# Two decoder layers on one core: slots by age, later low parts of the value weights, fp32r transposes of gathered rows

## The chip, the core and the metric

The kernel runs on one core of one Trainium2 chip. The core has a matmul engine (TensorE, PE in the profile, with its weight loads as PEld), a vector engine (VectorE, DVE), an activation engine (ScalarE, ACT), GpSimd (POOL) and a queue engine (SyncE, SP) that only issues DMAs here. The metric is the device time of one execution in microseconds. Three executions of the kernel before took 1535.93, 1536.97 and 1539.32 us; their median, 1536.97 us, is the time before.

## What is computed

Two layers over 512 tokens of width 1024. Each layer mixes tokens by two attentions that run on the same projection, and then sends each token through 2 of 16 experts:

```python
for l in range(DEPTH):
    mix = token_mixer(x, w_in[l], ...)      # selected sparse attention + stick-breaking attention
    x = layer_norm(DN_ALPHA * x + mix, ln1_g[l], ln1_b[l])
    ffn = grouped_moe(x, w_router, router_bias, exp_w_gate[l], exp_w_up[l], exp_w_down[l])
    x = layer_norm(DN_ALPHA * x + ffn, ln2_g[l], ln2_b[l])
...
def grouped_moe(...):
    scores = sigmoid(xf @ w_router)          # choose one group of 4 experts, then 2 of them
    for e in range(N_EXPERTS):
        h = silu(xf @ exp_w_gate[e]) * (xf @ exp_w_up[e])
        y = y + combine[:, e:e + 1] * (h @ exp_w_down[e])
```

All arithmetic is float32.

## The kernel before

**Products in three terms.** TensorE multiplies in the format fp32r, which holds fewer bits than float32. Each operand is therefore split in two (`Chip.split`): ScalarE copies it to an fp32r tile (the high part, line 484), and VectorE subtracts that from the original into a second fp32r tile (the low part, line 495). A product is three matmuls (`mm3`): low x high, high x low, high x high. So each weight tile of 128 x 1024 (two blocks of 512 columns, 512 KB) costs one DMA on SP, one ScalarE cast, one VectorE subtraction and its matmuls. The helpers record every operation, so in the profile nearly all VectorE work has line 495, all ScalarE casts line 484, all matmuls line 447 and all transposes line 445; tile names and times tell them apart. `s` are tiles in SBUF, `m` small ones (a few bytes per partition), `p` and `a` PSUM banks.

**The planner sets the order.** The program is first recorded as a list of operations with their dependencies (`Recorder.add`), each with an assumed duration and a priority, which is its place in the list, moved forward by `R.bump` for loads and splits of weights. `Recorder.plan` then simulates the five engines: at each step the engine that is free first takes the ready operation of the lowest priority number. The result is one order per engine, and the operations are emitted in it. A dependency that is added by hand (`o.deps.add`) acts in this simulation and so on the order; the emitted program waits only for what data and buffers need.

**Slots.** All working tiles share fixed slots: 48 in SBUF for kind `s`, 56 for `m`, 4 PSUM banks each for `p` and `a`. When an operation writes a new tile, `take` (in `plan`) picks a slot that is free at that time of the simulation. Before the change it is the one that came free last: `s` is sorted by the time of release, and the index is the largest one whose time has passed. In the emitted program the first writer of the new tile waits for the last users of the old tile in that slot, whenever they end on the chip. Groups have quotas: 46 slots for loads of expert weights (`x`), 24 for their split parts (`ew`), 2 for gathered rows (`xg`), 6 for their transposed parts (`xh`). The DMA queue SP works in order, so a load that waits for its slot holds back the loads behind it.

**A layer.** First come projections and the two attentions, then the output projection with the first normalisation and the router (`out_proj`, `route_tile`). The normalised rows go to DRAM (`x1d`), and a copy to `zd`, into which the experts add. Per expert (`moe`): GpSimd gathers the expert's rows from `x1d` (`gather`, line 1179) into a tile `xg`; TensorE transposes it in 8 blocks of 128 x 128 (`transpose_tile`, by an identity matrix `ident`); the 8 blocks are split; gate and up take 24 matmuls of 512 columns each (8 blocks in three terms), the two halves of down 12 each, 72 in all; GpSimd adds the scaled result to `zd` by an indirect DMA (`add_rows`, line 1184). Expert 0 has its rows from matmuls instead of a gather. Before the last expert stands a branch for overfull experts (`overflow`), not taken here, that reserves a number of tiles.

**Between the layers.** `ln2` reads `zd`, adds the last expert by matmuls, normalises the four tiles of 128 tokens, and transposes and splits each for the next layer (`x2t`). The first tile (t = 0) has its statistics from VectorE (`bn_stats`), the others from ScalarE. Meanwhile the next layer's first weights are loaded and split: those of the indexer (`indexer`) and the value weights of the second attention (`vb_by_tile`, four splits k2 = 0..3). In layer 1 the indexer and the value projection run tile by tile behind `ln2`.

Of the kernel before, what the change touches and what calls it, by code (L numbers as in the profile page):

```python
# [11 lines left out]
F = mybir.dt.float32  # L12
FR = mybir.dt.float32r
# [4 lines left out]
OP = mybir.AluOpType  # L18
# [4 lines left out]
P = 128  # L23
S = 512
D = 1024
# [28 lines left out]
class View:  # L54
# [19 lines left out]
    def real(self):  # L74
        x = self.buf.tile
        for f, a, k in self.chain:
            x = getattr(x, f)(*a, **k)
        return x
# [13 lines left out]
class Recorder:  # L92
# [82 lines left out]
    def plan(self):  # L175
# [93 lines left out]
        def take(o, t):  # L269
            for b in o.allocs:  # L270
                s = slots[b.kind]
                s.sort()
                i = max((j for j in range(len(s)) if s[j][0] <= t + 1e-9), default=0)
                b.slot = s.pop(i)[1]
                g = b.group
                if g is not None:
                    if live[g] >= self.QUOTA[g]:
                        heapq.heappop(glive[g])
                        live[g] -= 1
                    live[g] += 1  # L280
                    turn[g].pop()
# [3 lines left out]
        while done < len(self.ops):  # L285
            best = None
            for e in engs:
# [3 lines left out]
                t = free[e] if ready[e] else (pend[e][0][0] if pend[e] else None)  # L291
                if t is not None and (best is None or t < best[0]):
                    best = (t, e)
            if barrier and not any(p.prio < barrier[0].prio for e in engs for p in [x[3] for x in pend[e]] + [x[2] for x in ready[e]] if p.prio < barrier[0].prio):
                o = barrier.pop()
                t = max([o.ready] + [free[x] for x in engs if x != "SP"])
# [3 lines left out]
                t = w  # L300
                e = "ALL"
# [118 lines left out]
class Chip:  # L420
# [13 lines left out]
    def mm(self, out, terms, start, stop, transpose=None, also=()):  # L434
        dt = {F: 4, FR: 1, BF: 1}
        n = self.n(out)
        if transpose is not None:
            dur = 0.11
        else:
            dur = sum(max(dt[x.dtype if not isinstance(x, View) else x.ap.dtype] * n, 256) / 2400 + 0.004 for _, x in terms)  # L440

        def fn():
            o = real(out)
            if transpose is not None:
                self.nc.tensor.transpose(o, real(transpose[0]), transpose[1])  # L445
            for i, (w, x) in enumerate(terms):
                self.nc.tensor.matmul(o, real(w), real(x), start=start and i == 0, stop=stop and i == len(terms) - 1)  # L447
        reads = [x for t in terms for x in t] + ([transpose[0]] if transpose else [])
        o = self.r.add("PE", dur, fn, [out], reads, allocs=also)
        o.cols = sum(n * w.shape[0] / P for w, _ in terms) + n * (transpose is not None)  # L450
        o.cnt = sum(2 if (x.ap.dtype if isinstance(x, View) else x.dtype) == F else 1 for _, x in terms) + (transpose is not None)
        return o
# [91 lines left out]
def build(tc, x0, xT0, w_idx, w_main, w_br, w_out, w_exp, bgate, idxg, idxb,  # L544
          ln1g, ln1b, ln2g, ln2b, wrt, rbias, ln1c, hconst, tab0, out):
    nc = tc.nc
    with ExitStack() as ctx:
# [17 lines left out]
        C = Chip(R)  # L565


        ident = const.tile([P, P], F, name="ident")
        make_identity(nc, ident)
        identb = const.tile([P, P], BF, name="identb")  # L570
        nc.vector.tensor_copy(identb, ident)
        jp = const.tile([P, P], I32, name="jp")
# [28 lines left out]
        def s4(shape, dtype=F, group=None, reserve=0):  # L601
            return R.buf("s", shape, dtype, group, reserve)
# [10 lines left out]
        wr = const.tile([P, KD, NE], F, name="wr")  # L613
        rb = const.tile([P, NE], F, name="rb")
        lnc = const.tile([P, DEPTH, 2, KD], F, name="lnc")
        onesf = const.tile([P, P], F, name="onesf")
        nc.vector.memset(onesf, 1.0)
        loaded = []
        bias_t = const.tile([P, 256 + 384 + 512], BF, name="bias")
# [19 lines left out]
        def load_w(src, k0, n=512, group="raw", reserve=0, load="w", fine=False):  # L639
            t = s4([P, 2, n], F, group, reserve)  # L640
            if fine:
                for k in range(2):
                    C.dma(t[:, k, :], src[:, (k0 + k) * n:(k0 + k + 1) * n], P * 4 * n, load=load)
                return t
            C.dma(t, src[:, k0 * n:(k0 + 2) * n].rearrange("p (k n) -> p k n", k=2), P * 8 * n, load=load)
            return t

        def split_w(raw, n=512, group="w", after=None, fine=False):
            h = s4([P, 2, n], FR, group)
            w = s4([P, 2, n], FR, group)  # L650
            if fine:
                for k in range(2):
                    C.split(h[:, k, :], w[:, k, :], raw[:, k, :])
                return [(h[:, i, :], w[:, i, :]) for i in range(2)]
            o = C.split(h, w, raw)
            if after is not None:
                o.deps.add(after)
            return [(h[:, i, :], w[:, i, :]) for i in range(2)]
# [17 lines left out]
            for n in range(2):  # L676
                C.stt(dst[:, half(n)], dst[:, half(n)], rstd, b[:, half(n)], OP.mult, OP.add)

        def transpose_tile(src, dst_of):
            for hb in range(2):  # L680
                ps = bank("a")
                for k in range(4):
                    c = (hb * 4 + k) * P
                    C.tr(ps[:, k * P:(k + 1) * P], src[:, c:c + P], ident)
                dst_of(hb, ps)

        def proj_tok(l, xT, c, done, before=None):
# [255 lines left out]
        def vb_by_tile(l, xT, vt):  # L943
            R.bump += BUMP
            w = []
            for k2 in range(4):
                w += split_w(load_w(w_main[l, M_VB, k2 // 2], 2 * (k2 % 2)), group="wo")
            R.bump -= BUMP

            def tile_of(t):  # L950
                ts = slice(t * P, (t + 1) * P)
                ps = bank("p")
                for k in range(KD):
                    C.mm3(ps, xT[k][0][:, ts], xT[k][1][:, ts], *w[k], k == 0, k == KD - 1)
                evac_v([ps], vt)
            return tile_of
# [220 lines left out]
        def gather(dst, idx, also, skip):  # L1177
            kw = dict(bounds_check=S - 1, oob_is_err=False) if skip else {}
            R.add("POOL", 1.04, lambda: nc.gpsimd.indirect_dma_start(  # L1179
                out=real(dst), out_offset=None, in_=x1d, in_offset=IOA(ap=real(idx), axis=0), **kw),  # L1180
                [dst], [idx], rtok=[f"x1{t}" for t in range(NT)], nbytes=P * (2048 if skip else 4096), allocs=also)
# [58 lines left out]
        def moe(l, tb, gl, mci, loads, xacc, until, routed):  # L1240
            def prep(e):
                xh, xl = s4([P, KD, P], FR, "xh"), s4([P, KD, P], FR, "xh")

                def dst(hb, ps):
                    ks = slice(hb * 4, hb * 4 + 4)
                    C.split(xh[:, ks, :], xl[:, ks, :], ps.rearrange("p (k t) -> p k t", k=4))
                if e == 0:
                    xg = s4([P, D], group="xg")
                    C.copy(xg[:, half(0)], xacc[0])
                    C.v("tensor_copy", xg[:, half(1)], xacc[1])  # L1250
                    transpose_tile(xg, dst)
                    return xh, xl
                xg = s4([P, D], group="xg")
                last = e == NE - 1
                gather(xg, gl[:, 0:1] if last else tb[:, e, 0:1], [xh, xl], not last)
                transpose_tile(xg, dst)
                return xh, xl

            def weights(e, i):
# [131 lines left out]
        def ln2(l, x2t, tail):  # L1391
            acc, oh, yo = tail
            R.bump += LNB
            lg, lb = load_ln(ln2g[l], ln2b[l])
            R.bump -= LNB
            for t in range(NT):
                ts = slice(t * P, (t + 1) * P)
                r = acc[t]
                ps = [bank("a" if x2t is None and t > 1 else "p") for _ in range(2)]
                for n in range(2):  # L1400
                    C.mm(ps[n], [(ident, r[:, half(n)])], True, False)
                for n in range(2):
                    C.mm(ps[n], [(oh[:, t, :], y[:, half(n)]) for y in yo], False, True)
                if t:
                    mean, rstd = stats_by_act(r, ps)
                else:
                    bs, mv = sm([P, 2, 6]), sm([P, 2])
                    for n in range(2):
                        C.v("bn_stats", bs[:, n, :], ps[n], n=512)
                    rstd, mean = norm_of(mv, bs, LN_EPS / ALPHA ** 2), mv[:, 0:1]  # L1410
                for n in range(2):
                    C.stt(r[:, half(n)], ps[n], mean, lg[:, half(n)], OP.subtract, OP.mult)
                for c in (half(0), half(1)) if t == 0 else (slice(0, D),):
                    C.stt(r[:, c], r[:, c], rstd, lb[:, c], OP.mult, OP.add)
                C.dma((out if l == DEPTH - 1 else x2d)[ts, :], r, P * 4096, wtok=[f"x2{t}"])
                if x2t is not None:
                    def dst(hb, ps):
                        for k in range(2):
                            h, w = x2t[hb * 2 + k]
                            C.split(h[:, :, ts], w[:, :, ts], ps[:, k * 256:k * 256 + 256].rearrange("p (k t) -> p k t", k=2))  # L1420
                    transpose_tile(r, dst)

        def x_tiles():
            x2 = [(s4([P, 2, S], FR), s4([P, 2, S], FR)) for _ in range(KD // 2)]
# [165 lines left out]
```

## Time and profile before

| | |
|---|---|
| median of three executions | 1536.97 us |
| the profiled execution | 1539.54 us |
| its span, first to last instruction | 1537.7 us |
| mean granted TensorE clock | 0.983 |
| read from HBM, written | 293.80 MB, 28.46 MB |
| loads of expert weights | 384 of 512 KB |
| gathers, scatter-adds | 30, 30 |

How it is read: a row of a timeline has the start in us from the span's start, its length in us, engine, line, operation, output <- inputs, shape and count, and in brackets the idle time of the engine before it and what ended that. A row of groups has count, busy us and mean ns of one, then the idle time before. A row of waits reads "engine, output, line <- what it waited for: us in total, times, longest". A row of stretches has busy us and number of instructions for PE, PEld, DVE, ACT and POOL, then the granted clock, the DMA share and GB/s. Neighbouring instructions of one kind are merged in a timeline, so that a row can hold several with their count.

The layers lie in the span as follows: attention of layer 0 to about 360 us, projection and routing to 470, experts to 745; layer 1 attention to about 1120, projection and routing to 1225, experts to 1510; the last normalisation to the end.

### The profile page before, as it was taken

Reading aid. Unit: us, or ns where it says so; the run is one execution under the profiler, and the core shown is the slowest. Engines: PE = TensorE matmul, PEld = TensorE weight load, DVE = VectorE, ACT = ScalarE, POOL = GpSimd, SP = SyncE. Lnnn points to the kernel's source line nnn. Section 1 sums busy time; section 2 is a strip of 40 time slices with the busy share of each in tenths; the row PEclk is TensorE's granted clock in tenths of the full one; section 3 lists DMA queues with packets and bytes.
Section 4 is the critical chain, followed back from the end, with each engine's and each line's share of the span. In section 5 each row is a group of like instructions: output and inputs, shape, how many; then the busy total and the mean of one; then the engine's idle time right before and its main releaser. Section 6 shows DMA issues by size and latency. Waiting matters only on the chain. (4 is left out here: it accounts for less than half of the span.)

```text
span 1537.7 us, 21018 instructions
## 1 busy us (share of the span) xinstructions
PE 1475.2 (96%) x7188; PEld 1178.9 (77%) x7188; DVE 1249.5 (81%) x2301; ACT 896.6 (58%) x1459; POOL 142.4 (9%) x127
## 2 busy tenths in 40 slices
PE   8999999999989999999799999999999899999985
PEld 7877777777867878888588777777778578888874
DVE  5699996777587989999765999867766789999975
ACT  4335543675146878888623455446831478888873
POOL 0000000000031131210010000000001212112110
PEclk9999999999999999999999999999999899999998
DMA  6221112117888989999712221221287889999962
GB/s 217 71 91 57 68 56 89 63 42 288 302 280 297 337 309 348 341 334 333 237 61 69 83 61 50 82 83 55 70 306 279 302 307 351 341 352 339 351 216 108
DMA packets 91265, 308.52 MB, mean 201 GB/s; under 512 B 15439, under 2 KB 15567, under 8 KB 91152
## 3 DMA queue, kind: packets, MB, share of 16 engines
q1 hardware_dynamic: 82000, 290.69, 53.5%
q0 software_dynamic: 9152, 16.43, 4.5%
q8 instruction: 58, 0.95, 0.2%
q14 instruction: 55, 0.45, 0.1%
HBM read 293.80 MB, written 28.46 MB: 210 GB/s over the span
## 5 line engine op out<-in xcount | busy, mean ns | idle before, releaser
L447 PE MATMUL p<-s,s 128*128 128x512 f32 (+1 forms) x5192 | 1268.1, 398 | 28.1 <-DVE s L495 25.7
L447 PEld LDWEIGHTS p<-s,s 128*128 128x128 f32 x5192 | 952.9, 191 | 234.9 <-DVE s L495 25.5
L495 DVE TENSOR_TENSOR s<-s,s 128x1024 fp32r<-128x1024 f32 (+2 forms) x526 | 612.1, 1195 | 152.4 <-ACT s L484 112.3
L484 ACT CAST s<-s 128x1024 fp32r<-128x1024 f32 (+2 forms) x526 | 518.2, 1029 | 226.6 <-PE p L447 141.6
L495 DVE TENSOR_TENSOR s<-a,s 128x256 fp32r<-128x256 f32 (+3 forms) x386 | 169.5, 479 | 36.5 <-ACT s L484 32.7
L484 ACT CAST s<-a 128x256 fp32r<-128x256 f32 (+2 forms) x354 | 127.1, 414 | 109.8 <-PE a L445 103.7
L445 PE MATMUL a<-ident,s 128*128 128x128 f32 x888 | 134.0, 277 | 13.5 <-DMA s<-x1d,m 6.4
L445 PEld LDWEIGHTS a<-ident,s 128*128 128x128 f32 x888 | 106.7, 142 | 44.9 <-issue 11.5
L523 POOL TENSOR_TENSOR m<-m,nhalf 128x1 f32<-128x1 f32 x24 | 17.8, 741 | 891.0 <-DVE m L495 881.6
L480 ACT ACTIVATE s<-a 128x512 f32<-128x512 f32 (+3 forms) x156 | 61.9, 450 | 46.0 <-PE a L447 27.5
L484 ACT COPY s<-a 64x512 f32<-64x512 f32 (+1 forms) x48 | 27.8, 583 | 96.7 <-PE a L445 45.3
L1184 POOL DMA_INDIRECT zd<-s,m x30 | 61.1, 2035 | 199.8 <-ACT s L487 167.4
L487 ACT ACTIVATE s<-p,m 128x512 f32<-128x512 f32 (+1 forms) x64 | 44.1, 689 | 53.5 <-PE p L447 50.6
L1179 POOL DMA_INDIRECT s<-x1d,m x30 | 43.6, 1452 | 267.9 <-PE p L447 220.2
L464 PE MATMUL a<-s,s 64*128 64x384 f32 (+3 forms) x456 | 67.4, 351 | 0.0
L447 PEld LDWEIGHTS a<-s,s 128*128 128x128 f32 x360 | 57.0, 188 | 9.2 <-issue 2.2
L447 PE MATMUL a<-s,s 128*128 128x324 f32 (+4 forms) x360 | 62.2, 321 | 1.5 <-DVE s L495 1.3
L464 PEld LDWEIGHTS a<-s,s 64*128 64x128 f32 x456 | 41.3, 185 | 27.6 <-issue 20.4
L495 DVE MAX8 m<-s 128x8 f32<-128x256 f32 (+2 forms) x96 | 53.4, 556 | 1.8
L495 DVE MATCH_REPLACE8 s<-m,s 128x256 f32<-128x256 f32 (+2 forms) x96 | 52.0, 542 | 0.0
L495 DVE TENSOR_TENSOR_SCAN s<-s 128x128 f32<-128x128 f32 (+3 forms) x64 | 51.0, 812 | 0.1
L484 ACT CAST s<-p 128x512 fp32r<-128x512 f32 x48 | 27.9, 588 | 38.5 <-DVE p L495 22.7
(107 smaller groups left out, 632.4 us busy)
## 6 DMA issues: line engine op xcount, KB each, us to landing
s<-in_w_exp SPq DMA_DIRECT2D x384, 512.0 KB
s<-in_w_main SPq DMA_DIRECT2D x79, 512.0 KB
s<-in_w_br SPq DMA_DIRECT2D x16, 512.0 KB
s<-in_w_out SPq DMA_DIRECT2D x16, 512.0 KB
x1d<-s SPq DMA_DIRECT2D x8, 512.0 KB
zd<-s SPq DMA_DIRECT2D x8, 512.0 KB
s<-zd SPq DMA_DIRECT2D x8, 512.0 KB
s<-in_w_idx SPq DMA_DIRECT2D x8, 324.0 KB
```

The costliest lines, as they stand in the source:

```text
L445: self.nc.tensor.transpose(o, real(transpose[0]), transpose[1])
L447: self.nc.tensor.matmul(o, real(w), real(x), start=start and i == 0, stop=stop and i == len(terms) - 1)
L464: self.nc.tensor.matmul(real(o), real(t[i][0]), real(t[i][1]), start=i == 0, stop=stop and i == len(t) - 1)
L480: self.nc.scalar.activation(real(out), real(src), func, bias=real(bias), scale=real(scale), **kw)
L484: return self.r.add("ACT", 0.1 + self.psum(out, src) + self.n(out) * 0.833e-3, lambda: self.nc.scalar.copy(real(out), real(src)), [out], [ ...
L487: return self.r.add("ACT", 0.2 + self.n(out) * 0.833e-3, lambda: self.nc.scalar.mul(real(out), real(src), real(c)), [out], [src, c])
L495: getattr(self.nc.vector, method)(real(out), *[real(a) for a in args], **{k: real(x) for k, x in kw.items()}, **({} if accum is None else ...
L523: return self.r.add("POOL", 0.47, lambda: self.nc.gpsimd.tensor_tensor(real(out), real(a), e, OP.pow), [out], [a])
L1179: R.add("POOL", 1.04, lambda: nc.gpsimd.indirect_dma_start(out=real(dst), out_offset=None, in_=x1d, in_offset=IOA(ap=real(idx), axis=0), * ...
L1184: rows = R.add("POOL", 1.04, lambda: nc.gpsimd.indirect_dma_start(out=zd, out_offset=IOA(ap=real(idx), axis=0), in_=real(src), in_offset=None,
```

## The change

Three edits, and a constant that goes with the third:

- `take` uses the slot that has been free longest (index 0 of the sorted list) for every kind but `m`.
- In `vb_by_tile` the low parts of the value weights k2 = 1, 2, 3 depend on the last operation of the first tile's normalisation in `ln2`, kept in the list `first_tile`.
- The gathered rows are written to an fp32r tile (as raw float32 bytes), and their transposes use an fp32r identity; the PSUM output is viewed in the same type. All other transposes use the same bytes viewed as float32.
- The identity is made in the buffer `onesf`, copied by VectorE to the fp32r tile, and `onesf` is set to ones afterwards.

```diff
@@ take
-                i = max((j for j in range(len(s)) if s[j][0] <= t + 1e-9), default=0)
+                i = max((j for j in range(len(s)) if s[j][0] <= t + 1e-9), default=0) if b.kind == "m" else 0
@@ mm
-                self.nc.tensor.transpose(o, real(transpose[0]), transpose[1])
+                self.nc.tensor.transpose(o.bitcast(transpose[1].dtype), real(transpose[0]), transpose[1])
@@ constants
-        ident = const.tile([P, P], F, name="ident")
-        make_identity(nc, ident)
+        onesf = const.tile([P, P], F, name="onesf")
+        make_identity(nc, onesf)
+        identr = const.tile([P, P], FR, name="identr")
+        nc.vector.tensor_copy(identr, onesf)
+        ident = identr.bitcast(F)
...
-        onesf = const.tile([P, P], F, name="onesf")
         nc.vector.memset(onesf, 1.0)
@@ transpose_tile
-        def transpose_tile(src, dst_of):
+        def transpose_tile(src, dst_of, by=ident):
...
-                    C.tr(ps[:, k * P:(k + 1) * P], src[:, c:c + P], ident)
+                    C.tr(ps[:, k * P:(k + 1) * P], src[:, c:c + P], by)
@@ vb_by_tile
                 w += split_w(load_w(w_main[l, M_VB, k2 // 2], 2 * (k2 % 2)), group="wo")
+                if k2:
+                    R.ops[-1].deps.add(first_tile[-1])
@@ moe, prep
-                xg = s4([P, D], group="xg")
+                xg = s4([P, D], FR, group="xg")
                 last = e == NE - 1
-                gather(xg, gl[:, 0:1] if last else tb[:, e, 0:1], [xh, xl], not last)
-                transpose_tile(xg, dst)
+                gather(xg.bitcast(F), gl[:, 0:1] if last else tb[:, e, 0:1], [xh, xl], not last)
+                transpose_tile(xg, dst, identr)
@@ ln2
                 for c in (half(0), half(1)) if t == 0 else (slice(0, D),):
-                    C.stt(r[:, c], r[:, c], rstd, lb[:, c], OP.mult, OP.add)
+                    o = C.stt(r[:, c], r[:, c], rstd, lb[:, c], OP.mult, OP.add)
+                if t == 0:
+                    first_tile.append(o)
...
+        first_tile = []
```

## The prediction, made before the change was run

> **What bounds the kernel now.** I read the page first, then busy times by stretches, then the waits, then the timeline around each long wait.
>
> ```profile
> PE 1475.2 (96%) x7188; PEld 1178.9 (77%) x7188; DVE 1249.5 (81%) x2301; ACT 896.6 (58%) x1459; POOL 142.4 (9%) x127
> ```
>
> TensorE (PE) is busy for 96% of the 1537.7 us span, so time is won in two ways only: work taken off PE, or PE stalls taken away. A stretch inside the experts of layer 0 shows how closely the others follow (busy us of PE, PEld, DVE, ACT, POOL; then granted clock, DMA share, GB/s):
>
> ```profile
> 560.00:580.00 20.00, 20.00 (x86) 16.39 (x85) 17.60 (x18) 16.03 (x20) 3.57 (x2) 0.88 0.88 292
> ...
> 600.00:620.00 20.00, 20.00 (x96) 16.70 (x95) 18.75 (x19) 17.32 (x21) 4.56 (x3) 1.00 0.98 347
> ```
>
> In the steady state PE has no idle time, DVE 1.25 us in 20, and the DMA engines are full as well. The first row is the same work with the clock at 0.88. Three stretches show where that comes from:
>
> ```profile
> 557.90:564.80 6.90, 6.24 (x15) 4.88 (x16) 6.39 (x6) 6.80 (x9) 2.05 (x1) 0.51 0.63 218
> 742.30:745.70 3.40, 2.94 (x16) 2.54 (x14) 3.22 (x4) 1.68 (x3) 0.00 (x0) 0.50 0.77 278
> 1496.60:1503.40 6.80, 3.49 (x15) 3.19 (x15) 4.19 (x5) 2.94 (x3) 0.00 (x0) 0.50 0.22 77
> ```
>
> After a stall PE runs at half clock for 3.4 or 6.8 us, so a stall costs more than its gap. What the stalls wait for:
>
> ```profile
> ACT s L484 <- DMA zd<-s,m: 17.0, 10, 6.6
> ```
> ```profile
> SPq L526 <- DVE s L495: 816.8, 213, 34.8
> ```
>
> The first row (us in total, times, longest): ScalarE, about to write the high part of a weight, waits for a scatter-add into zd. No weight depends on zd; what can tie the two is the SBUF slot: the planner gives out the slot that came free last, and that slot's last user is still being read by the scatter, or is tied to it. The second row is the DMA queue's own: nearly every load is held by a slot that VectorE has only just let go.
>
> **The change, part by part.** *Slots by age.* No instruction is added or moved by this; each new tile takes the slot that has been free longest in the plan, so its wait is for older work. Three stalls carry the gain. The first:
>
> ```profile
> 556.21 2.94 ACT L484 CAST s<-s 128x1024 fp32r<-128x1024 f32 x3 [6.64 <-DMA zd<-s,m]
> ...
> 557.30 0.50 PE L447 MATMUL p<-s,s 128*128 128x512 f32 x1 [1.81 <-ACT s L484]
> ```
>
> ScalarE stands 6.64 us and PE loses 1.81. The half clock behind it lets 6.24 us of busy time do 0.51 of its work: 6.24 x 0.49 = 3.06. Together 4.9. The second and the third:
>
> ```profile
> 739.72 1.23 DVE L495 TENSOR_TENSOR s<-s,s 128x1024 fp32r<-128x1024 f32 x1 [3.15 <-DMA zd<-s,m]
> ...
> 741.33 3.48 PE L447 MATMUL p<-s,s 128*128 128x256 f32 x18 [3.87 <-DVE s L495]
> ```
> ```profile
> 1498.12 3.68 DVE L495 TENSOR_TENSOR s<-s,s 128x1024 fp32r<-128x1024 f32 x3 [6.45 <-DMA zd<-s,m]
> ...
> 1499.40 3.36 PE L447 MATMUL p<-s,s 128*128 128x256 f32 x14 [5.12 <-DVE s L495]
> ```
>
> At 741 the low part could start once its high part is cast; I give PE 2.6 of the 3.87 us, and of the half clock 2.94 x 0.5 = 1.5: 4.1. At 1499 VectorE was free 6.45 us earlier, more than PE's gap, so all 5.12 go, and 3.49 x 0.5 = 1.75 of clock: 6.9. Sum 15.9. Ends: 0 if the wait is a dependency and not the slot, 17.1 with the whole 3.87. I take nearly the upper end, since a weight's split has no data from zd. What is late next is the split itself, then the load. The loads cost PE nothing directly: they may only be issued earlier. Tiles of kind m keep the old rule.
>
> The Trainium skill (TensorE: Matmul & The Clock Gate, "What's actually happening") gives the half clock to an idle 3413 ns window; the three rows agree in length and depth. By its rule the clock terms (6.3 of the 15.9) return only where no such window stays idle; without them the sum is 6.3 smaller.
>
> *fp32r transposes.* 30 gathers (15 experts, 2 layers) give 8 transposes each, 240 of the 888. Their pace now, in a group of 12 (4 of another kind and these 8), against single durations:
>
> ```profile
> 585.89 1.47 PE L445 MATMUL a<-ident,s 128*128 128x128 f32 x12
> 603.57 1.47 PE L445 MATMUL a<-ident,s 128*128 128x128 f32 x12
> ```
> ```profile
> L445 PE MATMUL a<-ident,s 128*128 128x128 f32 x888 | 134.0, 277 | 13.5 <-DMA s<-x1d,m 6.4 <-DVE s L495 4.8 <-DVE m L495 0.9
> L445 PEld LDWEIGHTS a<-ident,s 128*128 128x128 f32 x888 | 106.7, 142 | 44.9 <-issue 11.5 <-DVE s L495 9.6 <-DMA s<-x1d,m 3.4
> ...
> L447 PE MATMUL a<-s,s 128*128 128x384 f32 x64 | 16.4, 337 | 0.0
> ...
> L447 PE MATMUL a<-s,s 128*128 128x256 f32 x64 | 12.8, 282 | 0.0
> ```
> ```profile
> 407.91 0.96 PE L447 MATMUL a<-k,s 128*128 128x16 f32 x8
> ```
>
> Pace: (1470 - 277) / 11 = 108 ns. A transpose of 128 columns lasts 277 ns, as long as an fp32r matmul of 256 columns (282): fp32 streams its identity twice. One pass of 128 columns is 337 - 282 = 55 ns. The other limit is the weight load. The router's 16-column matmuls, which stream next to nothing, still come about 0.1 us apart, so an ordinary four-byte load takes that long; the transposes' loads are shorter (142 ns). Lower end: one pass, about 58 ns. Upper end: the fp32r transpose's load is an ordinary one, and the pace stays 108 (or 112, a loss of 1 us in all). I take 58, because the transpose's load is already of the short kind. In each 8 the last is followed by an ordinary load that binds anyway, so 7 count: 30 x 7 x 50 ns = 10.5 us, all on PE, which has no idle time there.
>
> The same page ("Terms") calls transpose mode four times faster for FP32. The trace does not show that at 108 ns, twice one pass of 55; if the fp32r identity brings it out, the term would be 30 x 7 x 53 ns = 11.1.
>
> *Low parts after the first tile.* Three VectorE subtractions of the next value weights move behind the first tile's last step; no DMA goes with them, and the dependency is in the plan alone, so nothing waits on a new semaphore.
>
> ```profile
> 755.68 1.21 DVE L495 TENSOR_TENSOR s<-s,s 128x1024 fp32r<-128x1024 f32 x1
> ...
> 758.65 1.17 DVE L495 TENSOR_TENSOR s<-s,s 128x1024 fp32r<-128x1024 f32 x1
> ...
> 759.81 1.40 DVE L495 SCALAR_TENSOR_TENSOR s<-p,m,s 128x512 f32<-128x512 f32 x2
> ...
> 765.71 2.48 PE L447 MATMUL a<-s,s 128*128 128x324 f32 x15 [1.33 <-DVE s L495]
> ...
> 772.89 4.92 PE L447 MATMUL p<-s,s 128*128 128x512 f32 x21
> ```
>
> The first and the last of the three are shown, 1.2 us each. They stand between the first tile's statistics and its normalisation (759.81): 3.6 us. Between 0 (latencies fill the room) and 3.6 comes back at the index matmul of 765.71; below nothing, one of them in front of the transposed tile's split costs 1.2. I take 2.0. Their own reader is the matmul at 772.89, 7 us after that one: this hides them. If that cover were gone, 1.2 us each would be paid.
>
> The extra identity copy at the start is one small VectorE operation while it waits for the first loads: nothing, or at most itself.
>
> *Sum.* 15.9 + 10.5 + 2.0 = 28.4, less 1.0 that the loads may take back (second rival): 27.4. The profiled execution took 1539.54 (span 1537.7 and 1.8 around it), 2.57 above the median of 1536.97. 1539.54 - 27.4 = 1512.1; on the median's footing 1509.5.
>
> **The rivals.** *No faster transpose:* the load binds at 108 ns. For it stand the router's matmuls, against it the 142 ns. 1509.5 + 10.5 = 1520.
>
> *The loads become the bound:*
>
> ```profile
> q1 hardware_dynamic: 1763, 6.41, 87.9%
> ```
>
> This row is of 600 to 620: 6.41 MB in 20 us at a DMA share of 0.98. An expert needs 12 x 512 KB = 6.29 MB, so 19.6 us, while PE takes 17.7 (603.57 - 585.89). PE already eats into a lead. If that lead is nearly gone, what is saved among the experts (10.5 + 4.9) is waited for again, and 741, 1499 and the boundary stay: 4.1 + 6.9 + 2.0 = 13.0, so 1524. Against it: no PE wait on an expert load stands among the waits, and 560 to 580 (DMA at 0.88 behind the stall) fills up again. The Trainium skill (DMA: Bandwidth & Descriptors, "Where 436 GB/s comes from") puts a core's HBM limit at about 358 GB/s; the 347 above agree, and no earlier issue would lift them.
>
> *Slower: the gathers come late.* Free slots let the queue run ahead, more loads are in flight, and each gather shares the engines with them.
>
> ```profile
> 593.12 1.04 POOL L1179 DMA_INDIRECT s<-x1d,m  x1 [9.73 <-PE p L447]
> ```
> ```profile
> DMA to landing us min/median/max: 5.7/6.8/7.8
> ```
>
> A gather is issued 603.57 - 593.12 = 10.4 us before its transposes and lands after 6.8. From 10.4 on, each microsecond costs 30; from about 11.3 the gain is used up. At 12 us: 30 x 1.6 = 48 more, 1557. Against it: the engines are full now as well, and the gathers, held 9.73 us by a slot, start earlier too.
>
> *It does not do what it says:* zd is waited for in earnest and the transposes keep their pace: 2 us of gain less 1, 1536.
>
> **How the numbers follow.** Forecast 0.55 (1500 to 1517 by its terms' ends), no faster transpose 0.22, loads 0.11, no change 0.05, slower 0.07. A measurement of this kernel can tell about 0.2%, 3 us, from no change. The range 1500 to 1527 takes in the first three. Faster 0.88, same 0.05, slower 0.07.
>
> **What would show it.** Right: no wait on zd left in ScalarE's and VectorE's rows; the clock at 1.00 in the experts; group of 12 in about 1.1 us; the index matmul of the second layer without its 1.33 us; most loads no longer held by VectorE. Wrong: the group still 1.47; PE waiting for loads of expert weights or for gathers; a stall of 5 us before the last expert's last matmuls; the low parts in front of the transposed tile's split.

## The result, and the profile after

Four executions of the changed kernel took 1510.46 to 1514.59 us, median 1514.01, beside 1538.14 for four of the kernel before: a ratio of 0.9836 (95% interval 0.981 to 0.9862). The forecast was 1509.5, its range 1500 to 1527. The profiled execution took 1514.59 (span 1512.9), 24.95 us less than the 1539.54 of before; the sum of the forecast was 27.4.

The busy times on the page of the changed kernel, then three stretches from its view by windows:

```profile
PE 1464.2 (97%) x7188; PEld 1172.2 (77%) x7188; DVE 1242.4 (82%) x2302; ACT 890.9 (59%) x1459; POOL 142.0 (9%) x127
```
```profile
560.00:580.00 20.00, 20.00 (x97) 16.65 (x96) 18.71 (x19) 17.39 (x22) 3.73 (x2) 1.00 0.99 356
600.00:620.00 20.00, 20.00 (x96) 16.67 (x95) 18.71 (x21) 17.30 (x22) 3.87 (x3) 1.00 1.00 361
...
735.10:738.50 3.40, 3.40 (x8) 2.75 (x9) 2.49 (x4) 0.78 (x2) 0.00 (x0) 0.50 0.94 362
```

The experts now run at a clock of 1.00; at the layer boundary (735) a half clock is left. The waits for `zd`, and the DMA queue's own waits:

```profile
POOL s L1183 <- DMA zd<-s,m: 38.9, 5, 8.1
...
ACT s L484 <- DMA zd<-s,m: 9.1, 5, 2.2
...
DVE s L495 <- DMA zd<-s,m: 1.7, 2, 0.9
```
```profile
SPq L526 <- PE p L447: 564.6, 249, 18.7
SPq L526 <- DVE s L495: 359.1, 124, 14.5
```

ScalarE's longest wait for `zd` is now 2.2 us in place of 6.6, but the ties are not gone: the gathers on GpSimd now wait 38.9 us for `zd`, where it was one wait of 9.2. The queue's waits for VectorE fell from 213 to 124, and 249 are now for a matmul, which reads the slot after the split (172 before). PE's timeline, at the places that the prediction named:

```profile
579.79 1.23 PE L445 MATMUL a<-identr,s 128*128 128x128 f32 x12
...
597.27 1.23 PE L445 MATMUL a<-identr,s 128*128 128x128 f32 x12
...
730.27 2.42 PE L447 MATMUL p<-s,s 128*128 128x256 f32 x18 [0.51 <-DVE s L495]
...
733.70 0.41 PE L445 MATMUL a<-identr,s 128*128 128x128 f32 x2 [0.79 <-DVE s L495]
735.08 7.34 PE L447 MATMUL p<-s,s 128*128 128x512 f32 x24 [0.97 <-DVE s L495]
...
749.93 1.98 PE L447 MATMUL p<-s,identr 128*128 128x512 f32 x4 [2.21 <-DVE s L495]
...
754.70 2.49 PE L447 MATMUL a<-s,s 128*128 128x324 f32 x15 [0.98 <-DVE s L495]
...
1478.95 2.06 PE L447 MATMUL p<-s,s 128*128 128x256 f32 x15 [0.51 <-DVE s L495]
```

The stall of 5.12 us at 1499 is 0.51 here (1478.95). That of 3.87 at 741 is 0.51 (730.27). The two waits of the first tile, 2.46 and 1.33 before, are still 2.21 and 0.98. A group of 12 transposes lasts 1.23 in place of 1.47, and the experts' period is 597.27 - 579.79 = 17.48 in place of 17.68. The last six of the eight that the change made fp32r start 82 to 87 ns apart (597.83 to 598.25), the first four of a group, which it did not touch, 108. The first tile's wait in the kernel before, which the prediction does not show:

```profile
760.60 1.98 PE L447 MATMUL p<-s,ident 128*128 128x512 f32 x4 [2.46 <-DVE s L495]
```

Both kernels issue 7188 matmuls, in orders that differ only locally, so the n-th matmul of one trace can be set beside the n-th of the other. The difference of their starts steps where time is won. The same was done for four experiments, each a profiled execution against that of before (us; minus is earlier; stretches left out hold up to 2.3 us each, so the columns don't add up to the span):

| stretch, in times of before | forecast | changed | age alone | old rule, GpSimd's slots last | fp32r alone | low parts alone |
|---|---|---|---|---|---|---|
| 363 to 399 (a stall at 366) | 0 | +1.6 | +1.6 | +1.6 | +1.6 | +1.6 |
| 529 to 568 (stall at 557) | -4.9 | -6.3 | -6.0 | -6.1 | -6.2 | -5.5 |
| 568 to 725 (9 experts) | -3.2 | -1.8 | 0.0 | 0.0 | -1.8 | 0.0 |
| 725 to 767 (741, low parts) | -6.1 | -3.3 | -0.3 | -0.2 | +2.9 | -0.2 |
| 1121 to 1158 | 0 | -1.65 | 0.0 | 0.0 | 0.0 | -1.65 |
| 1250 to 1264 (a stall at 1258) | 0 | -2.1 | -2.1 | -1.8 | +1.2 | -0.2 |
| 1358 to 1485 (7 experts) | -2.5 | -1.4 | 0.0 | 0.0 | -1.4 | 0.0 |
| 1485 to 1523 (stall at 1499) | -6.9 | -7.0 | -7.0 | -7.0 | -0.2 | +3.4 |
| whole span | -27.4 | -24.8 | -19.2 | -16.9 | -4.9 | -4.6 |

Two rows already speak against a reading of the profile of before: the 6 us at 557 are gone in all five traces, also in the two that leave the slots alone, and the stall at 366 costs 1.6 us more in all five. One row was not in the forecast at all, a fourth stall that goes with each change of the slot rule and stays without one. In the trace of before:

```profile
1258.27 4.08 PE L447 MATMUL p<-s,s 128*128 128x512 f32 x15 [1.91 <-DVE s L495]
```

The table explains these profiled executions and not wholly the medians. If the 6 us at 557 were only in the one profiled execution of before, the medians should differ by some 19 us; they differ by 24.1, and by 23.5 in the later run of the changed kernel. So the other executions of the kernel before lose some 5 us that its one trace, the slow scatter-add left out, does not show. Where they lose them stays open.

### The profile page after: what moved, and what is told of

It reads as the page before. It is cut to its first block, busy times and chain, and to the rows that moved or that the text cites. A ratio compares the mean times of both kernels' runs of the same rounds, so it can differ in the third digit from the quotient of the medians.

```text
span 1512.9 us, 20946 instructions
## 1 busy us (share of the span) xinstructions
PE 1464.2 (97%) x7188; PEld 1172.2 (77%) x7188; DVE 1242.4 (82%) x2302; ACT 890.9 (59%) x1459; POOL 142.0 (9%) x127
## 5 line engine op out<-in xcount | busy, mean ns | idle before, releaser
L495 DVE TENSOR_TENSOR s<-s,s 128x1024 fp32r<-128x1024 f32 (+1 forms) x526 | 606.7, 1192 | 86.2 <-ACT s L484 75.6
L484 ACT CAST s<-s 128x1024 fp32r<-128x1024 f32 (+1 forms) x526 | 515.5, 1034 | 68.0 <-PE p L447 29.9
L445 PE MATMUL a<-identr,s 128*128 128x128 f32 x888 | 123.3, 268 | 12.1 <-DVE s L495 5.9
L445 PEld LDWEIGHTS a<-identr,s 128*128 128x128 f32 x888 | 101.1, 140 | 41.3 <-issue 13.5
L523 POOL TENSOR_TENSOR m<-m,nhalf 128x1 f32<-128x1 f32 x24 | 19.2, 802 | 876.5 <-DVE m L495 871.2
L1188 POOL DMA_INDIRECT zd<-s,m x30 | 55.4, 1848 | 253.6 <-ACT s L487 185.3
L1183 POOL DMA_INDIRECT s<-x1d,m x30 | 47.3, 1576 | 204.3 <-PE p L447 88.4
```

The source lines that it names most:

```text
L445: self.nc.tensor.transpose(o.bitcast(transpose[1].dtype), real(transpose[0]), transpose[1])
L484: return self.r.add("ACT", 0.1 + self.psum(out, src) + self.n(out) * 0.833e-3, lambda: self.nc.scalar.copy(real(out), real(src)), [out], [ ...
L495: getattr(self.nc.vector, method)(real(out), *[real(a) for a in args], **{k: real(x) for k, x in kw.items()}, **({} if accum is None else ...
L523: return self.r.add("POOL", 0.47, lambda: self.nc.gpsimd.tensor_tensor(real(out), real(a), e, OP.pow), [out], [a])
L1183: R.add("POOL", 1.04, lambda: nc.gpsimd.indirect_dma_start(out=real(dst), out_offset=None, in_=x1d, in_offset=IOA(ap=real(idx), axis=0), * ...
L1188: rows = R.add("POOL", 1.04, lambda: nc.gpsimd.indirect_dma_start(out=zd, out_offset=IOA(ap=real(idx), axis=0), in_=real(src), in_offset=None,
```

## The experiments

Theory A: age pays by breaking ties between a weight's slot and an earlier user of that slot, at 741 and 1499; a transpose is paced by its weight load, 84 ns; what is left at the boundary is VectorE's order. Rivals: the gain of age is general (loads run ahead); the loads take the transposes' gain back. A kernel whose edit adds lines has its line numbers moved by up to 11.

**Slots by age alone** (6 executions).
```diff
-                i = max((j for j in range(len(s)) if s[j][0] <= t + 1e-9), default=0)
+                i = max((j for j in range(len(s)) if s[j][0] <= t + 1e-9), default=0) if b.kind == "m" else 0
```


> Slots by age alone, for all kinds but m; transposes and low parts as before. Theory A (three stalls): the gain is that of the three stalls at 557, 741 and 1499 (4.9, 4.1 and 6.9 us in the forecast), so some 13 to 16 us less than the kernel before, and the profile has no wait of ScalarE or VectorE for zd at these places. Rival B (no dependency broken): with only the slots changed the waits for zd come back elsewhere and less than 5 us are gained. Rival C (the gain is general: loads and splits run further ahead everywhere): 18 us or more, and the gain grows steadily over the span instead of in three steps.

Measured: 1517.49 against 1536.51, ratio 0.9874 (0.985 to 0.9898), 19 us less. That is above theory A's 13 to 16 and at rival C's 18, but the table shows steps, not a steady growth: 6.0 at 557, 7.0 at 1499, 2.1 at 1258, 0.0 through the experts. At 741 the stall shrinks, but a half clock that follows later eats it.

**The old rule, with the slots of GpSimd and of the branch last** (6 executions).
```diff
-                i = max((j for j in range(len(s)) if s[j][0] <= t + 1e-9), default=0)
+                i = max((j for j in range(len(s)) if s[j][0] <= t + 1e-9), key=lambda j: (not held.get((b.kind, s[j][1])), j), default=0)
...
+                    held[b.kind, b.slot] = o.eng in ("ALL", "POOL")
```


> The kernel before with one change of the slot rule: still the slot that came free last, but among the free ones those whose last user was a GpSimd operation (the scatter-adds) or the overflow branch are taken only if there is no other. The order of the operations is exactly that of the kernel before. Theory A: the three stalls are tied to just these slots, so this rule gains nearly what age gains, 11 to 16 us, and the three stalls are gone. Rival C: age helps because every slot is older; then this rule gains under 5 us and VectorE still holds most loads.

Measured: 1520.39, ratio 0.9889 (0.9864 to 0.9915), 16 us less, its interval overlapping that of age. The queue still waits 212 times for VectorE, so the gain is not one of earlier loads. Its waits, and ScalarE, then PE, at the stall of 741:

```profile
ACT s L486 <- DMA zd<-s,m: 1.9, 1, 1.9
```
```profile
731.90 0.73 ACT L486 CAST s<-s 128x648 fp32r<-128x648 f32 x1 [4.43 <-DMA s<-in_w_idx]
```
```profile
735.70 3.56 PE L449 MATMUL p<-s,s 128*128 128x256 f32 x18 [3.52 <-DVE s L497]
```

At 1499 the 7.0 us are won whole, and at 1258 the 1.8: the tie to a slot that GpSimd or the branch had held is shown to be the cause there (which of the two, this rule does not separate). At 741 hardly anything is won although no wait for `zd` is left there: ScalarE now stands 4.43 us for an indexer weight of the next layer, with the last expert's casts queued behind it. The first of these loads is issued at 722.26 here and at 712.38 in the changed kernel, 9.9 us earlier, while PE is only 2.4 us ahead there at this place. With age alone it is issued at 711.80. So here it seems to be the general effect, rival C, that counts; no run moved this load by itself.

**fp32r transposes alone** (12 executions), with the change's edits of `mm`, the constants and `transpose_tile` that this needs.
```diff
-                xg = s4([P, D], group="xg")
+                xg = s4([P, D], FR, group="xg")
...
-                gather(xg, gl[:, 0:1] if last else tb[:, e, 0:1], [xh, xl], not last)
-                transpose_tile(xg, dst)
+                gather(xg.bitcast(F), gl[:, 0:1] if last else tb[:, e, 0:1], [xh, xl], not last)
+                transpose_tile(xg, dst, identr)
```

> The fp32r transposes of the gathered rows alone; order of the operations exactly that of the kernel before. Theory L (the transposes' weight load paces them, about 84 ns, as the changed kernel's trace shows): (108 - 84) x 8 x 30 = 5.8 us less than before, so a ratio of about 0.9962. The forecast's own pace of 58 ns: 10.5 us, ratio 0.9932. Rival: the saved time is eaten by the loads of expert weights, ratio above 0.998.

Measured: 1532.75, ratio 0.9979 (0.996 to 0.9998). The interval just holds theory L's 0.9962 and not the forecast's 0.9932. The trace is sharper: 0.2 us per expert, so 30 x 0.2 = 6.0, and no load took any of it back:

```profile
600.04 1.23 PE L445 MATMUL a<-identr,s 128*128 128x128 f32 x12
617.53 1.23 PE L445 MATMUL a<-identr,s 128*128 128x128 f32 x12
```

This kernel has the order and the slots of before, and still no stall at 557. The scatter-add and ScalarE's cast behind it, in the trace of before (the first fence; the cast was shown above with its wait of 6.64) and here:

```profile
540.28 7.45 POOL L1184 DMA_INDIRECT zd<-s,m  x1 [5.03 <-ACT s L487]
```
```profile
543.36 1.77 POOL L1186 DMA_INDIRECT zd<-s,m  x1 [5.04 <-DMA s<-in_w_exp]
```
```profile
553.19 2.00 ACT L484 CAST s<-s 128x1024 fp32r<-128x1024 f32 x2 [0.55 <-DMA zd<-s,m]
```

In the profiled execution of before this one scatter took 7.45 us to issue, where the median of its 30 was 1.79; here it took 1.77 and the wait was 0.55. With the low parts alone, again with the same slots, it took 1.77 and the wait was 0.31. The tie is real; the 6 us at this place hang on that one slow scatter-add.

**Low parts alone** (12 executions), with the change's edits of `ln2` that fill `first_tile`.
```diff
                 w += split_w(load_w(w_main[l, M_VB, k2 // 2], 2 * (k2 % 2)), group="wo")
+                if k2:
+                    R.ops[-1].deps.add(first_tile[-1])
```

> The low parts of the three value weights behind the first tile's normalisation alone. Forecast: 2.0 us less than before, all of it between 755 and 775, the index matmuls of layer 2 start without the 1.33 us wait for VectorE. Rival: latencies fill the room, nothing changes (within 0.5 us at 770). Second rival: the low parts land in front of the transposed tile's split, up to 1.2 us slower.

Measured: 1534.49, ratio 0.9967 (0.9948 to 0.9987). PE at the first tile, then the stretch ahead of it by windows:

```profile
757.53 1.88 PE L447 MATMUL p<-s,ident 128*128 128x512 f32 x4
759.25 1.04 PE L445 MATMUL a<-ident,s 128*128 128x128 f32 x8
760.04 1.18 PE L447 MATMUL p<-s,s 128*128 128x512 f32 x4
761.06 3.36 PE L447 MATMUL a<-s,s 128*128 128x324 f32 x21
```
```profile
736.30:749.90 13.60, 11.45 (x36) 9.32 (x37) 8.84 (x12) 5.11 (x8) 0.00 (x0) 0.50 0.87 291
```

Neither of the first tile's waits is left: 2.46 and 1.33, 3.8 us, more than the 2.0 of the forecast and its upper end of 3.6. That the table shows only -0.2 is the half clock, which in this execution held for 13.6 us behind the stall of 741.

**All four low parts** (5 executions, and 5 more below). In the changed kernel, VectorE at the first tile:

```profile
746.34 1.23 DVE L495 TENSOR_TENSOR s<-s,s 128x1024 fp32r<-128x1024 f32 x1 [2.42 <-ACT s L484]
747.48 1.29 DVE L495 BATCH_NORM_STATS2 m<-p 128x6 f32<-128x512 f32 x2
...
751.90 1.21 DVE L495 TENSOR_TENSOR s<-s,s 128x1024 fp32r<-128x1024 f32 x1
...
753.10 1.21 DVE L495 TENSOR_TENSOR s<-s,s 128x1024 fp32r<-128x1024 f32 x1
754.23 1.07 DVE L495 TENSOR_TENSOR s<-a,s 128x256 fp32r<-128x256 f32 x3
```

The low part that the change did not move (k2 = 0) waits for its cast and that for its load, with the first tile's statistics queued behind it.
```diff
-                if k2:
-                    R.ops[-1].deps.add(first_tile[-1])
+                R.ops[-1].deps.add(first_tile[-1])
```


> The changed kernel with the low part of the first value weight (k2 = 0) behind the first tile's normalisation as well. Theory A: in the changed kernel that one low part waits 2.42 us for its load and holds up the statistics of the first tile behind it on VectorE (746.34 against 747.48), which is PE's wait of 2.21 us at 749.93; moved, that wait goes and with it 2 to 3 us: about 1511.5. Rival: the bank that PE waits for is freed late anyway (ScalarE's or the loads' time), the 2.21 us stay, nothing is gained. Other side: the fourth low part stands in front of the transposed tile's split, PE's 0.98 us at 754.70 grow by up to 1.2 us.

Measured: 1507.61, ratio 0.9825 (0.9808 to 0.9842). The second profiled execution of this kernel, PE and VectorE at the first tile:

```profile
743.64 1.88 PE L447 MATMUL p<-s,identr 128*128 128x512 f32 x4
745.36 1.04 PE L445 MATMUL a<-identr,s 128*128 128x128 f32 x8
746.15 1.18 PE L447 MATMUL p<-s,s 128*128 128x512 f32 x4
747.16 3.36 PE L447 MATMUL a<-s,s 128*128 128x324 f32 x21
```
```profile
740.72 1.30 DVE L495 BATCH_NORM_STATS2 m<-p 128x6 f32<-128x512 f32 x2 [0.72 <-PE p L447]
```

Both waits are gone, and the index matmuls follow without a gap. The stretch is 5.2 us shorter than in the changed kernel's profile, in both executions: 3.2 are the waits, the rest is the half clock at 735, which did not follow here. In the second profile of the changed kernel (below) it did not follow either, and there the waits are 2.70 and 0.98 and the stretch 4.1 us longer than here. So the waits are worth 3 to 4 us in both pairs of profiles, and the clock goes either way.

**Four low parts behind the transposed tile's split** (6 executions).
```diff
-                if t == 0:
-                    first_tile.append(o)
...
                     transpose_tile(r, dst)
+                if t == 0:
+                    first_tile.append(R.ops[-1])
```

> As the kernel before this in the list, but the four low parts depend on the last operation of the first tile's split behind its transposes. Theory A: besides the 2.21 us also the 0.98 us wait at 754.70 goes, in which PE waits for a split that stands behind two low parts: 3 to 4 us less than the changed kernel, about 1510.5. Rival: the low parts are now late for their own reader, the value projection some 10 us later, and PE waits there for up to 4 x 1.2 us.

Measured: 1510.61, ratio 0.9839 (0.9817 to 0.9861): no better. Both waits are gone here too, so the 0.98 needed no later place. Set beside the kernel with four low parts, its profile loses 2.2 us to a half clock that followed at 735, and 2.0 at the first gathers of layer 1 (1.48 us of wait in the changed kernel):

```profile
1207.74 2.10 PE L445 MATMUL a<-identr,s 128*128 128x128 f32 x12 [4.72 <-DMA s<-x1d,m]
```

**Late scatter-adds, before and changed** (one execution each, so that the steps of the traces count and not the totals).
```diff
-            rows = R.add("POOL", 1.04, lambda: nc.gpsimd.indirect_dma_start(
+            calls.append(0)
+            now = LATER if len(calls) % 15 in range(1, 11) else 0
+
+            def late():
+                for _ in range(now):
+                    nc.gpsimd.memset(idle, 0.0)
+
+            rows = R.add("POOL", 1.04, lambda: late() or nc.gpsimd.indirect_dma_start(
```


> The kernel before, with 16 small fills of a tile that nobody reads ahead of ten of the fifteen scatter-adds of each layer on GpSimd, each scatter some 4 to 5 us later. Theory A (a cast is tied to a scatter-add by its slot, and the stall at 557 is that tie with a scatter that took 7.45 us to issue in place of 1.8): the stall shows in every run and at several experts, ScalarE's waits for zd rise from 17 us in all to over 40, and the experts of layer 0 (500 to 710) take 5 to 30 us longer. Rival (the stall at 557 has nothing to do with the scatter's time): no more than 1 us.

> The changed kernel with the same fills ahead of the same scatter-adds. Theory A: slots given out by age are older than the scatter by many microseconds, so the delay costs the experts of layer 0 less than 1 us, and ScalarE's waits for zd stay under 12 us. Rival: the delay costs the changed kernel as much as the kernel before.

Measured: 1545.11 and 1520.17, each some 6 to 10 us above its own kernel's median. ScalarE and VectorE in the kernel before, then VectorE and PE in the changed one:

```profile
ACT s L487 <- DMA zd<-s,m: 21.1, 11, 4.1
DVE s L498 <- DMA zd<-s,m: 18.9, 5, 6.5
```
```profile
500.45 2.36 DVE L498 TENSOR_TENSOR s<-s,s 128x1024 fp32r<-128x1024 f32 x2 [4.87 <-DMA zd<-s,m]
```
```profile
501.73 12.59 PE L450 MATMUL p<-s,s 128*128 128x512 f32 x47 [3.62 <-DVE s L498]
```

Theory A holds in kind and fails in size. Against the kernel with the low parts alone, which has the same slots and no slow scatter, the late scatters cost the experts of layer 0 5.3 us, in four steps (1.6, 1.1, 1.7 and 0.8). The changed kernel loses 4.3 us in one step, at 501.7, and nothing from there to the end of layer 0's experts. So age leaves one tie with less than 5 us of slack, early in the experts, and loosens the later ones. ScalarE's 21.1 us stay under the 40 expected; in the changed kernel its waits for `zd` are 13.6 us, above the 12 expected. The fourth stall is such a tie too: in the kernel before it grows from 1.91 to 3.94 us (at 1257.93), behind a wait of VectorE for `zd` of 3.78.

**One more transpose, with half the load or half the stream** (one execution). Each extra transpose writes again what its neighbour has just written.
```diff
+                    if (len(halves) - 1) // 4 % 2 == 0:
+                        self.nc.tensor.transpose(o2[:64, :], s[:, :64], by)
+                    else:
+                        self.nc.tensor.transpose(o2[:, :64], s[:64, :], by[:64, :64])
```


> The changed kernel with one more fp32r transpose behind each of the 240, into the same place: in the first group of four, of 64 columns of the rows (half the weight load, all 128 columns streamed); in the second group, of 64 partitions with a quarter of the identity (a load of 128 columns, half the columns streamed). Theory L (the weight load paces them): a pair with half a load takes clearly less than 2 x 84 ns, towards 126, and a pair with half the stream stays near 168. Theory S (streaming or writing paces them): the other way round, near 168 with half a load and towards 126 with half a stream. If both come out near 2 x 84, the pace is one of instructions, whatever their size.

Measured: 1546.33 in all. PE in one group; L450 are the transposes of the kernel, L454 the extra ones with half the load, L456 those with half the stream:

```profile
625.40 0.22 PE L454 MATMUL a<-identr,s 128*64 128x128 f32 x1
625.46 0.24 PE L450 MATMUL a<-identr,s 128*128 128x128 f32 x1
625.54 0.23 PE L454 MATMUL a<-identr,s 128*64 128x128 f32 x1
...
625.91 0.24 PE L456 MATMUL a<-identr,s 64*128 64x64 f32 x1
626.08 0.28 PE L450 MATMUL a<-identr,s 128*128 128x128 f32 x1
626.29 0.25 PE L456 MATMUL a<-identr,s 64*128 64x64 f32 x1
```

A pair with half a load takes 0.14 us (625.40 to 625.54), not 0.168: theory L. Both of its transposes stream all 128 columns, so streaming does not pace the 84 ns. The other half of the test tells nothing: with 64 partitions a pair takes 0.38 us (625.91 to 626.29), so something else sets in.

**SBUF slots alone by age; the changed kernel again; four low parts again** (5 executions each, on one chip).
```diff
-... if b.kind == "m" else 0
+... if b.kind != "s" else 0
```


> The kernel with all four low parts moved, and slots by age for SBUF tiles (kind s) alone; PSUM banks go back to the one that came free last. Order of the operations exactly the same. Theory A: the gain of age lies in SBUF slots, so the time is within 2 us of that kernel, near 1508. Rival: the banks carry part of it, 3 us or more slower, with new PE waits for VectorE in the attention.

> The changed kernel itself, beside the two that build on it: 1512 to 1515.

> The kernel with all four low parts moved, once more beside the changed kernel: 3 to 7 us less than it, if the gain seen at 735 to 760 (5.2 us in one profile, of which 3.2 are PE's two waits and the rest a half clock that did not follow) stands in every run; 3 us if the half clock comes back in some.

Measured: 1507.73 (0.9825, 0.9801 to 0.9848), 1512.88 (0.9857, 0.9832 to 0.9882) and 1507.35 (0.9825, 0.9801 to 0.985). The PSUM banks carry none of the gain of age that these times can show. With four low parts the kernel is 5.5 us faster than the changed one here. The intervals of the ratios still touch, but all in all its ten executions took 1505.56 to 1510.83, the nine of the changed kernel 1510.46 to 1514.59: this version beats both kernels.

## Why the prediction was right, and where not

The direction, the range and the likeliest case held. The point was 2.5 us too far between the two profiled executions (4.5 from the median of 1514.01), the balance of these steps: 27.4, less 4.5 for the transposes and 2.8 at 741 and the first tile, plus 1.2 at 557, 0.1 at 1499, 1.0 that the loads did not take and 2.4 elsewhere, is 24.8. That the sum came so near is in part luck: 6.1 of the 24.8 hang on one slow scatter-add, and the 2.4 come from places that the prediction does not name. Of its signs of being right the clock in the experts and the loads came; the waits for `zd` did not go (9.1 and 1.7 us left), the group takes 1.23 us for some 1.1, and the index matmul still waits 0.98.

*The stall at 1499: right.* Forecast 6.9, measured 7.0, in age alone and in the rule that only sets aside the slots of GpSimd and of the branch. "What can tie the two is the SBUF slot" is shown for this place, and for 1258, which "Three stalls carry the gain" leaves out. "Nearly every load" was too much for the queue's 213 waits for VectorE: 172 were for a matmul already.

*The stall at 741: right in the sum of its waits, wrong in cause and in clock.* PE waits 2.27 us there (0.51 + 0.79 + 0.97) where the three waits were 5.25, a gain of 3.0 for the 2.6 forecast. But the 1.5 of clock did not come in this execution: the row of 735.10 has 0.50. In the second profile of the changed kernel no half clock followed there. And the `zd` wait was only one of two: with it gone and the loads as late as before, an indexer weight's load keeps the stall. Age removes both; that it does so because the queue runs ahead is read from the times of issue.

*The stall at 557: the step that read one execution as the rule.* "ScalarE stands 6.64 us and PE loses 1.81 ... Together 4.9": the wait hung on one scatter-add that took 7.45 us to issue. The two runs with the same slots and without it wait 0.3 and 0.6 us, at no cost to PE. So the 6 us are in the difference of the two profiles and can't be counted on every time; that the medians fell as far as the profiles is not explained by this.

*fp32r transposes: the mis-sized term.* "I take 58, because the transpose's load is already of the short kind": the short load itself takes 84 ns at a stretch, above the one pass of 55 and under the 108 of before. (That the 108 are two passes stays the prediction's reading: the change alters the type of the rows and of the identity at once, so a slower load of float32 rows is not ruled out.) 30 x 8 x 24 ns = 5.8 by the pace, 6.0 by the trace, for 10.5. The lower end was priced from streaming, the upper end from another kind of load; the forecast did not ask what the short load costs where nothing else binds. The Trainium skill (TensorE: Matmul & The Clock Gate, "Back-to-back issue gap") gives about 81 ns for a stream of load and matmul pairs at 128 columns, against some 56 for the matmul alone; the 84 here agree, and the forecast had used only the matmul's price. The four times faster transpose of the same page ("Terms") shows nowhere.

*Low parts: right alone, mostly missing in the change.* Alone both waits go (3.8 us for the 2.0 forecast); in the change 3.19 of 3.79 us stay. The step that failed is "three VectorE subtractions ... move": the fourth stays, and in the changed kernel its load comes late (issued at 736.01 behind the reads of `zd`, landing at 745.24), so it stands where the three had stood. The last two low parts moved also stood in front of the transposed tile's split, the prediction's own condition for wrong, until all four were moved.

*Loads and gathers: the rivals did not come.* PE never waits for an expert weight, and the DMA share is 1.00 at 361 GB/s (0.98 and 347 before): the 1.0 us subtracted for it was not lost. The prediction's "no earlier issue would lift them" did not hold either: the five stretches of 20 us from 580 to 680 go at 360 to 364 GB/s, above the limit that it named, where they went at 338 to 347.

Two readings behind the rival of late gathers were wrong. The 6.8 and 7.8 us of landing come from 2 of the 30 gathers, since the trace of before holds no landing of the others. Low parts alone, with the gathers of before, has all 30, and the changed kernel too:

```profile
DMA to landing us min/median/max: 4.2/7.9/10.9
```
```profile
DMA to landing us min/median/max: 4.4/7.9/10.8
```

So the gathers land no later than before. And the gather of 593.12 is not read by the group of 603.57, which waits for the semaphore of the gather at 575.44, but by the next one, at 621.26. Its cover was 28 us and not 10.4, and the same gather of the changed kernel (582.75, read at 614.8) has 32. The bound of this rival lay much further off than the prediction put it, and the gathers' new waits for `zd` cost PE nothing among the experts.

The rest, some 2.4 us (24.8 less 6.1, 6.0, 3.3 and 7.0), is 2.1 at 1258 and the half clock at 1128 that did not follow in this execution (1.65), less the one at 366 that did (1.6); what is left is small.

## What to carry to other kernels

Before a stall of one profiled execution enters a sum, look at the length of the DMA issue that released it against the median of its group: a tie is worth what it costs in most executions. A split taken out of a critical chain leaves its siblings in place; ask of each one that stays when its load lands in the new order. A matmul that streams little can be paced by its load, so price both, each from a row in which it binds.

## What the runs showed of the hardware

**The half clock comes on a grid, and not after every stall.** In the trace of before the first six of its nine stretches begin at 435.06, 462.36, 557.94, 742.26, 1127.96 and 1196.23: 8, 36, 90, 203 and 223 times 3.413 us from the first. The Trainium skill (TensorE: Matmul & The Clock Gate, "What's actually happening") calls the window free-running; the traces agree: the first line of the grid behind the first instruction lies 0.1 to 3.2 us behind it, differently from execution to execution. The same stall of 1.81 us at 366 was followed by a half clock in 10 of 14 traces, at 1.6 us each. Before, then changed, first the stall and then the stretch behind it:

```profile
366.72 3.48 PE L447 MATMUL p<-s,s 128*128 128x512 f32 x14 [1.82 <-DVE s L495]
```
```profile
366.70:370.10 3.40, 3.38 (x15) 2.79 (x16) 3.40 (x5) 0.59 (x1) 0.00 (x0) 1.00 1.03 419
```
```profile
366.00 4.37 PE L447 MATMUL p<-s,s 128*128 128x512 f32 x11 [1.81 <-DVE s L495]
```
```profile
366.50:369.90 3.40, 3.40 (x9) 2.63 (x9) 3.40 (x6) 0.59 (x1) 0.00 (x0) 0.50 1.02 407
```

Its place on the grid sorts them, together with those of a second stall of 1.81 us, at 1127. Of these 28 stalls 12 have a line of the grid inside them, and no half clock followed; 16 lie whole between two lines, and in 15 the half clock began at the next line (in the 16th, the one of before at 366, the stall ended 0.07 us ahead of that line). So the idle window of 3413 ns that the prediction cites is not needed: 1.81 us idle in one window were enough. No run moved such a stall along the grid on purpose. A clock term belongs to an execution and is worth its share of executions.

**Transposes of 128 and of 64 partitions in turn are dear.** They cost 0.38 us a pair, against 0.14 for 128 and 64 columns of the rows in turn. The first pair differs in the columns streamed as well, so which of the two costs the time was not separated. The Trainium skill (TensorEngine Tiling (Array Packing), "Key Properties") says that a change of tiling mode drains the engine. That would fit the pair of 128 and 64 partitions, while no drain shows for the columns; no run shows which mode an instruction takes.

**One scatter-add of 420 took four times as long to issue** (30 in each of 14 traces): 7.45 us for a median of 1.79, and it cost that execution 6 us. No other took over 2.61.
